# One over the softmax sum moves from each query tile into its head pair's gate, and GpSimd's work is pinned to written order

## The chip, the cores and the metric

One core of one Trainium2 chip. The metric is device time in microseconds (us). Before: median 1193.33 us of 3 runs (1192.71 to 1193.87). Below, a tile is 128 queries of one head.

## What is computed

A two-layer trunk on x (1024 x 1024) with 256 memory tokens; each layer ends in x <- LayerNorm(alpha * x + W_out [main * silu(gate); mem * silu(gate)]). The change lies in layer 1, where main is forgetting attention (16 heads of width 64):

```
logits = einsum(q, k) * scale + (cum[t] - cum[s])      # cum: running sum of the log forget gates
p = softmax(where(s <= t, logits, -inf))               # per head, 8 blocks of 128 queries
main = p @ v                                           # per head, 1024 x 64
y = concat(main * silu(g_main), mem * silu(g_mem)) @ w_out
```

The factor 1/sum of the softmax belongs to a query of a head. It may be put on p before `p @ v`, or on the rows of main, or on the gate that multiplies main.

## The kernel before

Every f32 product on TensorE (PE) is made from 16-bit halves: a high half and a low half (the rest). The profile's name PE is TensorE, DVE is VectorE, ACT is ScalarE, POOL is GpSimd, SP issues most DMAs.

**The attention stage** (`fox`, about 636 to 1068 us of the span) walks 16 heads in pairs, and in each head 8 tiles, number 7 (1024 columns) down to number 0 (128 columns). Tiles 7 to 4 have two parts of at most 512 columns (a and b below), tiles 3 to 0 have one. One tile runs so:

- PE: two matmuls for each part (L321) write the logits into a bank of PSUM called L; there are three of these banks, taken in turn.
- DVE: one instruction for each part (L1007; the profile shows it as CUSTOM_DVE_ANT_0 and its reader, `order` lists print ISA) adds the forget rows R or a masked copy of them (raw), takes the row extremum, and frees the bank L.
- ACT: the exponential (L1015), with the row sum as a second output, into PSUM (tag T, two banks).
- DVE: `inverse_of`, 1/sum: L1025 or L1027 (a 128x1 tensor_scalar), then L1028 (a 128x1 reciprocal).
- ACT: the high half e/sum (L1043), which needs that 1/sum; DVE: the low half (L1044), which needs the high half.
- SP: DMA transposes of the halves (`turn`, L1060); six tiles later (LAG) PE multiplies them with the values (L1069), after every fourth tile (52 matmuls at i = 1 of the next head, 20 at i = 5), and ACT (L1086) and DVE (L1087) put the result into the pair's output tile G.

The instructions of one engine start in its order, so an instruction that waits holds all that stand behind it. DVE's order: the inverse of a tile is written behind the next tile's first part, its low halves behind the next tile's last part; a scheduler moves them from there.

**Fill.** Between logits and values PE gets matmuls of projections (L353, "slabs" of 48 matmuls of 512 columns: the next pair's keys, queries, values, and gates), spread evenly over the tiles of a pair by `Fill.pump`: PE should always have something to do. A slab's weights come by a 512 KB DMA into a tile B; GpSimd scales them (L174) and makes the halves (L191 high, L176 low), 512 columns at a time, two times a slab. The first step of a unit (its DMA) is asked when the unit before it begins.

**GpSimd** also makes the masked copies of the forget rows (L981, three tiles ahead), and multiplies a pair's output with its gate (`pair_out`, L1096, four of 128x256; `late_gate`, L1109, for pairs 3, 5, 6, whose gates are made late). Its order is the scheduler's.

**The last pair** (heads 14 and 15) has pieces of the output projection in its fill, whose halves are split by ACT (L196) and DVE (L197).

Of the kernel before, what the change touches and what calls it, by code (L numbers as in the profile page):

```python
# [9 lines left out]
F32 = mybir.dt.float32  # L10
# [32 lines left out]
class Fill:  # L43


    def __init__(self):
        self.units, self.left, self.due, self.early = [], 0, 0, []

    def add(self, units, cols, early=False):
        self.units.append(units)  # L50
        self.left += cols
        if early:
            self.early.append(units)

    def pump(self, cols):

        self.due += cols
        while self.due > 0 and self.units:
            if len(self.units) > 1 and self.units[1] in self.early:
                self.early.remove(self.units[1])  # L60
                next(self.units[1])
            n = next(self.units[0], None)
            if n is None:
                self.units.pop(0)
            else:
                self.due -= n
                self.left -= n
        if not self.units:
            self.due = self.left = 0
# [8 lines left out]
def trunk_kernel(ctx, tc, x, xT, memT, win, wk, wv0, wv, wmk, wmv, wout, poolw, pscale, lng, lnb, bforget, out):  # L78
# [94 lines left out]
    def gp_scaled_hi_lo(to, src, sc):  # L173
        nc.gpsimd.tensor_scalar(src, src, sc, 1.0, ALU.mult, ALU.mult)  # L174
        gp_copy(to.hi, src)
        nc.gpsimd.tensor_tensor(to.lo, src, to.hi, ALU.subtract)  # L176
# [146 lines left out]
    def slab(pieces_dram, X, evac, banks=("pj", 2), g=0):  # L323
# [9 lines left out]
        ws = list(pieces_dram) if arrived else [split_w(pieces_dram[0], [P, 4, P], sc, both[0])]  # L333
        accs = {}
# [455 lines left out]
    with tc.tile_pool(name="in1", bufs=1) as in1:  # L790
# [165 lines left out]
        def start_units(own, following):  # L956
# [11 lines left out]
            yield from islice(following, 48)  # L968
# [8 lines left out]
        def mask(hd, i, R):  # L977
# [3 lines left out]
            nc.gpsimd.affine_select(  # L981
                C[:, :w], R[:, lo:up], [[-1, w]], ALU.is_ge, -NEG, base=w - P, channel_multiplier=1,
            )
# [8 lines left out]

# [38 lines left out]
        joined = []  # L1031

        def halves(hd, i, es, r):

            L = (i + 1) * P
            if i in (2, 0):
                pair = joined.pop()[:, 2 * L + 2 * P :]
            else:
                pair = sb([P, 2 * S], "P", 4, F16)
                if i in (3, 1):  # L1040
                    joined.append(pair)
            for lo, up, e in es:
                nc.scalar.activation(pair[:, lo:up], e, AF.Copy, scale=r)  # L1043
                nc.vector.scalar_tensor_tensor(pair[:, L + lo : L + up], e, r, pair[:, lo:up], ALU.mult, ALU.subtract)  # L1044
            return hd, i, pair
# [46 lines left out]
        def pair_out(pr, c, o, g):  # L1092

            for k in (2 * c + 1, 2 * c) if g is not None else ():
                cols = slice(k * 2 * P, (k + 1) * 2 * P)
                nc.gpsimd.tensor_tensor(o[:, cols], o[:, cols], g[:, cols], ALU.mult)  # L1096
# [3 lines left out]
        def late_gate(pr):  # L1100
# [6 lines left out]
            for c in range(4):  # L1107
                cols = slice(c * 2 * P, (c + 1) * 2 * P)
                nc.gpsimd.tensor_tensor(o[:, cols], o[:, cols], g[:, cols], ALU.mult)  # L1109
            nc.sync.dma_start(y1d[pr // 4, :, pr % 4, :], o)  # L1110

        def fox(following, out_proj):
            fill, past, fresh = Fill(), [None] * LAG, [None]
            gs = {}
# [3 lines left out]

            def gate_ahead(pr):
                gs[pr] = G()  # L1120
                fill.add(gate_units(win[1, 12 + pr], gs[pr], X, 2), SLAB, True)
# [4 lines left out]
            for hd in range(HEADS + 1):  # L1126
# [3 lines left out]
                if hd < HEADS:  # L1130
                    if b == 0:
                        o, sums = G(), sb([P, 4 * ST], "sums", 2, F32, small).rearrange("p (n b i) -> p n b i", n=2, b=2)
                        if 0 < pr < 7:
                            for units in (k_units, q_units, v_units):
                                fill.add(units(pr + 1), SLAB, True)
                        for ahead in {0: (0, 1), 2: (2,), 4: (4,), 7: (7,)}.get(pr, ()):
                            gate_ahead(ahead)
                            if ahead == 0:
                                fill.add(following, SLAB)
                        for late in (3, 5, 6) if pr == 7 else ():  # L1140
                            fill.add(late_gate(late), SLAB, True)
                    R, ahead_R = ahead_R, None
                for i in range(ST if hd < HEADS else LAG):
# [7 lines left out]
                    def inverse():  # L1151
                        if fresh[0]:
# [3 lines left out]
                    def behind():  # L1156
                        if fresh[0]:
                            split.append(halves(*fresh[0]))
# [18 lines left out]
                    if hd < HEADS:  # L1177
                        new = (hd, tile_of, o)
                        fresh[0] = probs(hd, tile_of, R, sums, inverse, behind)
                    else:  # L1180
# [95 lines left out]
```

## Time and profile before

| | |
|---|---|
| runs | 1192.71, 1193.33, 1193.87 us |
| profiled execution, its own time | 1197.14 us |
| its span | 1195.3 us |
| PE busy | 1169.2 us, 98% of the span |
| DVE busy | 788.1 us, 66% |
| ACT busy | 685.2 us, 57% |
| GpSimd busy | 286.4 us, 24% |
| mean granted PE clock | 0.993 |

The profiled execution is 3.8 us above the median of the runs, and 1.8 us longer than its span. A busy engine is shown by the time of its instructions; matmuls overlap in the pipe, so the mean duration of one is longer than the distance between two. "Waited for" is idle time of an engine put down to the instruction that ended it.

### The profile page before, as it was taken

Reading aid. Unit: us, or ns where it says so; the run is one execution under the profiler, and the core shown is the slowest. Engines: PE = TensorE matmul, PEld = TensorE weight load, DVE = VectorE, ACT = ScalarE, POOL = GpSimd, SP = SyncE. Lnnn points to the kernel's source line nnn. Section 1 sums busy time; section 2 is a strip of 40 time slices with the busy share of each in tenths; the row PEclk is TensorE's granted clock in tenths of the full one; section 3 lists DMA queues with packets and bytes.
Section 4 is the critical chain, followed back from the end, with each engine's and each line's share of the span. In section 5 each row is a group of like instructions: output and inputs, shape, how many; then the busy total and the mean of one; then the engine's idle time right before and its main releaser. Section 6 shows DMA issues by size and latency. Waiting matters only on the chain. (4 is left out here: it accounts for less than half of the span.)

```text
span 1195.3 us, 19795 instructions
## 1 busy us (share of the span) xinstructions
PE 1169.2 (98%) x6941; PEld 673.1 (56%) x6941; DVE 788.1 (66%) x1840; ACT 685.2 (57%) x1512; POOL 286.4 (24%) x437
## 2 busy tenths in 40 slices
PE   8999999999999999999999999999999999999996
PEld 5556776555555557556674555555555545455553
DVE  6744675556765566447755888778877788874654
ACT  6468875966563234557431776666766667674210
POOL 3321001220000000010224454545434331750000
PEclk8999999999999999999999999999999999999999
DMA  7566557655286544446734889989996999785430
GB/s 259 167 228 210 152 115 214 222 190 159 88 281 169 146 134 121 136 130 125 179 146 121 185 181 210 206 173 189 209 185 139 168 193 206 201 195 174 173 109 36
DMA packets 286195, 203.88 MB, mean 171 GB/s; under 512 B 224912, under 2 KB 238352, under 8 KB 286096
## 3 DMA queue, kind: packets, MB, share of 16 engines
q1 hardware_dynamic: 279696, 181.59, 61.0%
q0 software_dynamic: 6400, 21.04, 5.4%
q8 instruction: 54, 0.88, 0.3%
q14 instruction: 45, 0.37, 0.1%
HBM read 116.01 MB, written 22.61 MB: 116 GB/s over the span
## 5 line engine op out<-in xcount | busy, mean ns | idle before, releaser
L353 PE MATMUL pj<-A,w 128*128 128x512 f16 (+2 forms) x2896 | 665.1, 383 | 2.8 <-DMA A<-A 1.1
L353 PEld LDWEIGHTS <-w 128*128 128x128 f16 (+1 forms) x2560 | 246.2, 98 | 280.3 <-issue 12.8
L1015 ACT ACTIVATE T<-MK,s 128x512 f32<-128x512 f32 x192 | 111.2, 579 | 66.5 <-DVE s L1007 50.0
L1044 DVE SCALAR_TENSOR_TENSOR P<-T,s,P 128x512 f16<-128x512 f32 x192 | 112.0, 613 | 39.4 <-ACT P L1043 38.2
L1043 ACT ACTIVATE P<-T,s 128x512 f16<-128x512 f32 x192 | 103.0, 576 | 53.5 <-issue 28.9
L174 POOL TENSOR_SCALAR B<-B,scales 128x512 f32<-128x512 f32 x54 | 39.5, 742 | 376.1 <-PE pj L353 262.5
L593 PEld LDWEIGHTS <-T 128*128 128x128 bf16 x736 | 70.8, 98 | 87.4 <-issue 4.4
L981 POOL TENSOR_SCALAR_AFFINE_SELECT raw<-R 128x256 f32<-128x256 f32 (+3 forms) x128 | 59.8, 469 | 132.8 <-DVE s L1007 70.8
L321 PE MATMUL L<-A 128*128 128x512 f16 (+3 forms) x384 | 84.8, 326 | 6.1 <-DVE s L1007 6.1
L197 DVE TENSOR_TENSOR w<-raw,w 128x512 bf16<-128x512 f32 x74 | 52.4, 709 | 56.3 <-ACT w L196 39.3
L353 PEld LDWEIGHTS pj<-A,w 128*128 128x128 f32 x352 | 65.2, 188 | 17.8 <-ACT w L196 2.3
L197 DVE TENSOR_TENSOR T<-T,T 128x1024 bf16<-128x1024 f32 x23 | 28.0, 1220 | 68.0 <-PE pj L593 38.3
L321 PEld LDWEIGHTS <-A 128*128 128x128 f16 x384 | 37.4, 98 | 49.4 <-issue 8.0
L176 POOL TENSOR_TENSOR w<-B,w 128x512 f16<-128x512 f32 x54 | 63.3, 1173 | 2.7
L196 ACT CAST w<-raw 128x512 fp32r<-128x512 f32 x76 | 46.7, 615 | 24.8 <-DMA raw<-in_win_dram 11.7
L196 ACT CAST T<-T 128x1024 fp32r<-128x1024 f32 x23 | 24.1, 1047 | 62.5 <-DMA T<-y1d 34.3
L1069 PEld LDWEIGHTS <-V 128*64 128x64 f16 (+1 forms) x1152 | 50.6, 104 | 12.9 <-issue 6.0
L1069 PE MATMUL O<-T,V 128*64 128x128 f16 (+1 forms) x1152 | 57.5, 220 | 0.0
L593 PE MATMUL pj<-B,T 128*128 128x512 bf16 (+1 forms) x192 | 53.0, 384 | 0.0
L1007 DVE CUSTOM_DVE_ANT_0 MK<-L,R,scales 128x512 f32<-128x512 f32 x64 | 45.3, 708 | 9.6 <-PE L L321 9.3
L198 ACT CAST w<-raw 128x512 bf16<-128x512 f32 x78 | 48.2, 618 | 5.7 <-PE pj L353 4.3
L593 PE MATMUL L<-B,T 128*128 128x512 bf16 (+1 forms) x168 | 47.3, 394 | 0.2 <-ACT T L198 0.2
(286 smaller groups left out, 1815.2 us busy)
## 6 DMA issues: line engine op xcount, KB each, us to landing
raw<-in_win_dram SPq DMA_DIRECT2D x66, 256.0 KB, 3.6
W<-in_win_dram POOLq DMA_DIRECT2D x48, 256.0 KB, 3.9
R<-cumd SPq DMA_DIRECT2D x16, 512.0 KB, 4.6
B<-in_win_dram SPq DMA_DIRECT2D x15, 512.0 KB, 4.5
y0d<-Y SPq DMA_DIRECT2D x12, 512.0 KB, 3.8
raw<-in_wout_dram SPq DMA_DIRECT2D x24, 256.0 KB, 2.7
T<-y0d SPq DMA_DIRECT2D x12, 512.0 KB, 4.5
A<-A SPq DMA_DIRECT2D x24, 256.0 KB, 4.5
```

The costliest lines, as they stand in the source:

```text
L176: nc.gpsimd.tensor_tensor(to.lo, src, to.hi, ALU.subtract)
L196: pin(nc.scalar.copy(to.hi, src))
L197: pin(nc.vector.tensor_tensor(to.lo, src, to.hi.bitcast(F32), ALU.subtract))
L198: pin((top or nc.scalar.copy)(to.top, src))
L321: nc.tensor.matmul(acc, a, b, start=i == 0, stop=i == len(terms) - 1)
L353: nc.tensor.matmul(accs[n], a[:, k, :], b[:, pc * 4 + k, n * NH : (n + 1) * NH], start=seen[n] == 1, stop=seen[n] == 3 * KT,)
L593: nc.tensor.matmul(accs[a][nh], y, w, start=kt == 8 and i == 0, stop=kt == 7 and i == 2,)
L981: nc.gpsimd.affine_select(C[:, :w], R[:, lo:up], [[-1, w]], ALU.is_ge, -NEG, base=w - P, channel_multiplier=1,)
L1015: nc.scalar.activation(e, p[:, lo:up], AF.Exp, bias=top, scale=-1.0, accum_out=sums[:, n, hd % 2, i : i + 1],)
L1043: nc.scalar.activation(pair[:, lo:up], e, AF.Copy, scale=r)
L1044: nc.vector.scalar_tensor_tensor(pair[:, L + lo : L + up], e, r, pair[:, lo:up], ALU.mult, ALU.subtract)
L1069: nc.tensor.matmul(acc[rows, (i % 4) * P : (i % 4) * P + P], v[:, b, 2 * j : 2 * j + (1 if e else 2), :].rearrange("p e d -> p (e d)"), pt ...
```

## The change

- **1/sum.** Heads 0 to 13 (pairs 0 to 6) no longer call `inverse_of`. The high half is e times a constant (PSCALE, 2^15), made by ACT at once behind the exponentials; the low half uses the same constant. So the pair's output is not yet divided by its sums. In the next pair's even head the sums of the pair (16 columns of 128) are added (L1072) and inverted (L1073) on DVE, transposed by PE into a bank of L (L1077), copied (L1079) and written to DRAM (8 KB, L1080); two reads (L1083) spread them over 64 partitions each, into a B tile I of 128 x 1024. GpSimd multiplies gate and I (L1236, four of 128x256) for pairs 0, 1, 2, 4; for pairs 3, 5, 6 I takes the place of the gate in `pair_out`, which had no product there before.
- **`pair_out`** and its write to DRAM move from the odd head's values to tile i = 7 of the next pair's even head. The last pair keeps its 1/sum in the tiles and its `pair_out` at the values.
- **GpSimd** keeps written order for masks, weight halves and products.
- **Weights** are asked in three stages (DMA; halves of the first 512 KB half; of the second), when the unit in front has 48 matmuls left, 30, and 16. The keys of the pair after the next (or gate 7) are asked in the odd head at i = 2, 5 and 6; gate 0 ahead of the stage.

GpSimd has 382 rows instead of 355 in its order, DVE 1550 instead of 1753, SP 480 instead of 469, and PE 7 matmuls (with their weight loads counted apart) more; the order of PE is otherwise the same.

```diff
     def pump(self, cols):
...
-            if len(self.units) > 1 and self.units[1] in self.early:
-                self.early.remove(self.units[1])
-                next(self.units[1])
-            n = next(self.units[0], None)
+            if len(self.units) > 1 and self.units[1][2]:
+                behind, ahead = self.units[0][1], self.units[1]
+                while ahead[2] > (2 if behind > 30 * NH else 1 if behind > 16 * NH else 0):
+                    next(ahead[0])
+                    ahead[2] -= 1
...
     def gp_scaled_hi_lo(to, src, sc):
-        nc.gpsimd.tensor_scalar(src, src, sc, 1.0, ALU.mult, ALU.mult)
-        gp_copy(to.hi, src)
-        nc.gpsimd.tensor_tensor(to.lo, src, to.hi, ALU.subtract)
+        pin = tc.keep_in_program_order
+        pin(nc.gpsimd.tensor_scalar(src, src, sc, 1.0, ALU.mult, ALU.mult))
+        pin(gp_copy(to.hi, src))
+        pin(nc.gpsimd.tensor_tensor(to.lo, src, to.hi, ALU.subtract))
...
+        def inverse_columns(sums):
+            nc.vector.tensor_tensor(sums[:, 0, :, 4:], sums[:, 0, :, 4:], sums[:, 1, :, 4:], ALU.add)
+            nc.vector.reciprocal(sums[:, 0], sums[:, 0])
+
+        def inverse_rows(pr, sums):
+            t = ps([P, NH], "L", 3)[: 2 * ST, :P]
+            nc.tensor.transpose(t, sums[:, 0].rearrange("p b i -> p (b i)"), ident)
+            rows = land([P, P])[: 2 * ST]
+            nc.vector.tensor_copy(rows, t)
+            nc.sync.dma_start(invd[2 * pr : 2 * pr + 2].rearrange("h (s q) -> (h s) q", s=ST), rows)
+            I = land([P, S])
+            for b in range(2):
+                nc.sync.dma_start(I[64 * b : 64 * b + 64], invd[2 * pr + b].partition_broadcast(64))
+            return I
...
                     def inverse():
-                        if fresh[0]:
+                        if fresh[0] and fresh[0][0] >= HEADS - 2:
...
+                    if b and pr < 7 and i in (2, 5, 6):
+                        if i == 2:
+                            head = k_units(pr + 2) if pr < 6 else gate_of(7)
+                        next(head)
...
                         fresh[0] = probs(hd, tile_of, R, sums, inverse, behind)
+                        if pr < 7:
+                            es = fresh[0][2]
+                            fresh[0] = hd, tile_of, es, PSCALE, high_halves(tile_of, es, PSCALE)
+                        if b == 0 and pr:
+                            if i == 0:
+                                inverse_columns(whole)
+                            if i == 1:
+                                I = inverse_rows(pr - 1, whole)
+                            if i == 6:
+                                g = gs.get(pr - 1)
+                                for k in range(4) if g is not None else ():
+                                    cols = slice(k * 2 * P, (k + 1) * 2 * P)
+                                    tc.keep_in_program_order(
+                                        nc.gpsimd.tensor_tensor(g[:, cols], g[:, cols], I[:, cols], ALU.mult))
+                                gs[pr - 1] = I if g is None else g
...
                         values(older[0], older[1] // 4, older[2])
-                        if older[0] % 2:
-                            pair_out(older[0] // 2, older[1] // 4, older[2], gs.get(older[0] // 2))
+                        if older[0] == HEADS - 1:
+                            pair_out(7, older[1] // 4, older[2], gs[7])
+                        elif older[0] % 2 and older[1] == 0:
+                            done = older[2]
+                    if b == 0 and i == 7:
+                        for c in (1, 0) if pr else ():
+                            pair_out(pr - 1, c, done, gs[pr - 1])
```

Two places of the order. First, DVE in head 2 (the even head of pair 1), from tile 6's second part to tile 5's second part; MK is the tile's logits, P holds the halves of tile 7, G the output of the pair before. Before:

```order
L1007 ISA MK_7056,s_7057<-L_7065,raw_6945,s_7057,scales 128x384
L1007 ISA s_7057 128x1
L1025 TENSOR_SCALAR s_7062<-sums_7004 128x1
L1028 RECIPROCAL s_7062<-s_7062 128x1
L1044 SCALAR_TENSOR_TENSOR P_7069<-T_7024,s_7062,P_7069 128x512
L1044 SCALAR_TENSOR_TENSOR P_7069<-T_7026,s_7062,P_7069 128x512
L1087 SCALAR_TENSOR_TENSOR G_6357<-O_7081,scales,G_6357 64x512
L1007 ISA MK_7142,s_7143<-L_7144,R_6688,scales 128x512
L1007 ISA s_7143 128x1
L1025 TENSOR_SCALAR s_7148<-sums_7004 128x1
L1007 ISA MK_7142,s_7143<-L_7151,raw_6973,s_7143,scales 128x256
```

The same piece in the changed kernel (L1024 is L1007's line there, L1067 is L1044's, L1128 is L1087's); P_6991 is tile 7, P_7034 tile 6:

```order
L1079 COPY B_7039<-L_7037 16x128
L1024 ISA MK_7018,s_7019<-L_7024,raw_6918,s_7019,scales 128x384
L1024 ISA s_7019 128x1
L1067 SCALAR_TENSOR_TENSOR P_6991<-T_6987,P_6991 128x512
L1067 SCALAR_TENSOR_TENSOR P_6991<-T_6989,P_6991 128x512
L1024 ISA MK_7107,s_7108<-L_7109,R_6676,scales 128x512
L1024 ISA s_7108 128x1
L1067 SCALAR_TENSOR_TENSOR P_7034<-T_7030,P_7034 128x512
L1128 SCALAR_TENSOR_TENSOR G_6369<-O_7048,scales,G_6369 64x512
L1024 ISA MK_7107,s_7108<-L_7113,raw_6944,s_7108,scales 128x256
```

The two inverses are gone; the values' L1128 now stands behind tile 5's first part, and tile 6's first low half (P_7034) stands between tile 5's two parts.

Second, GpSimd in pair 2, in the last three tiles of head 4, changed kernel. The raw rows are masks of head 5's tiles 7, 6 and 5; B_7930 is the values' weights of pair 3, w_7990 and w_8032 their halves; G_6371 is pair 1's gate, B_7753 its I, G_6970 its output:

```order
L1002 AFFINE_SELECT raw_7946<-R_7723 128x512
L1002 AFFINE_SELECT raw_7997<-R_7723 128x384
L176 TENSOR_SCALAR B_7930<-B_7930,scales 128x512
L1236 TENSOR_TENSOR G_6371<-G_6371,B_7753 128x256
L193 TENSOR_SCALAR w_7990<-B_7930 128x512
L1236 TENSOR_TENSOR G_6371<-G_6371,B_7753 128x256
L178 TENSOR_TENSOR w_7990<-B_7930,w_7990 128x512
L1236 TENSOR_TENSOR G_6371<-G_6371,B_7753 128x256 x2
L176 TENSOR_SCALAR B_7930<-B_7930,scales 128x512
L193 TENSOR_SCALAR w_8032<-B_7930 128x512
L1002 AFFINE_SELECT raw_8039<-R_7723 128x256
L178 TENSOR_TENSOR w_8032<-B_7930,w_8032 128x512
```

Before, in the same three tiles of head 4 (raw_8025, raw_8083 and raw_8119 are the masks of head 5's tiles 7, 6, 5). B_8178 is the weights of gate 2, which head 5's last tiles use; B_8577 those of pair 4's keys, used from head 6 on; B_10399 the values' weights of a later pair; G_7003 is pair 1's output, G_6360 its gate:

```order
L981 AFFINE_SELECT raw_8025<-R_7799 128x512
L176 TENSOR_TENSOR w_8445<-B_8178,w_8445 128x512
L981 AFFINE_SELECT raw_8083<-R_7799 128x384
L174 TENSOR_SCALAR B_10399<-B_10399,scales 128x512 x2
L1096 TENSOR_TENSOR G_7003<-G_7003,G_6360 128x256 x2
L981 AFFINE_SELECT raw_8119<-R_7799 128x256
L191 TENSOR_SCALAR w_8579<-B_8577 128x512
L981 AFFINE_SELECT raw_8155<-R_7799 128x256
L176 TENSOR_TENSOR w_8579<-B_8577,w_8579 128x512
```

Before, the halves in the queue at these tiles are those of the next slab but one and later ones; now they are those of the next slab (the values of pair 3, whose first matmuls stand in head 5's first tile), with the four new products of a gate between them.

More of the change, by code (lines that the diff above doesn't have):

```diff
@@ L954, in pair_units, with gate_of, ask, start_units @@
                 yield from v_units(p)
-        def start_units(own, following):
+        gs = {}
+        def gate_of(pr):
+            gs[pr] = G()
+            return gate_units(win[1, 12 + pr], gs[pr], X, 2)
+        def ask(units):
+            low[0] = True
+            next(units)
+            low[0] = False
+        def start_units(own, following, gate):
             yield from v_first()
```

77 lines of the change are left out of this document (46 added, 31 removed).

## The prediction, made blind

> **What bounds the kernel now.** I read the page's busy shares first, then the table of PE's waits for the whole run, then the same table for the attention stage alone (640 to 1030 us), and at last the timelines of the engines around two of the waits. The page's row of busy times, and the first row of PE's waits (total us, times, longest):
>
> ```profile
> PE 1169.2 (98%) x6941; PEld 673.1 (56%) x6941; DVE 788.1 (66%) x1840; ACT 685.2 (57%) x1512; POOL 286.4 (24%) x437
> PE L L321 <- DVE s L1007: 6.1, 7, 2.5
> ```
>
> PE is busy for 98% of the span (1195.3 us); no other engine passes 66%. So time on DVE, ACT or GpSimd counts only where PE waits for it. The largest such sum is that of the logits for a free bank L: 6.1 us in 7 waits, the longest 2.5. Nothing else that the change touches is among PE's waits of any size. The same table for the stage up to head 14:
>
> ```profile
> PE L L321 <- DVE s L1007: 3.5, 6, 1.1
> POOL raw L981 <- DVE s L1028: 47.8, 28, 4.3
> ```
>
> Six waits, 3.5 us, lie there; the seventh, 2.5, lies in the last pair. Now one of the six, in head 2 at 704 us: DVE, then ACT, then PE (start and duration in us; in brackets the idle time before and what ended it).
>
> ```profile
> 699.44 0.67 DVE L1007 CUSTOM_DVE_ANT_0 MK<-L,raw,s 128x384 f32<-128x384 f32 x1
> ...
> 700.40 0.21 DVE L1025 TENSOR_SCALAR s<-sums 128x1 f32<-128x1 f32 x1 [0.29 <-ACT T L1015]
> 700.65 0.16 DVE L1028 RECIPROCAL s<-s 128x1 f32<-128x1 f32 x1
> 701.90 1.41 DVE L1044 SCALAR_TENSOR_TENSOR P<-T,s,P 128x512 f16<-128x512 f32 x2 [1.08 <-ACT P L1043]
> 703.34 0.76 DVE L1087 SCALAR_TENSOR_TENSOR G<-O,scales,G 64x512 f32<-64x512 f32 x1
> 704.13 0.75 DVE L1007 CUSTOM_DVE_ANT_0 MK<-L,R,scales 128x512 f32<-128x512 f32 x1
> ...
> 699.55 0.69 ACT L1015 ACTIVATE T<-MK,s 128x512 f32<-128x512 f32 x1 [0.42 <-DVE P L1044]
> 700.18 0.19 ACT L1015 ACTIVATION_READ_ACCUMULATOR T<-MK,s 128x1 f32 x1
> 701.18 1.27 ACT L1043 ACTIVATE P<-T,s 128x512 f16<-128x512 f32 x2 [0.81 <-ACT T L1015]
> 702.47 0.68 ACT L1086 ACTIVATE G<-O,scales 64x512 f32<-64x512 f32 x1
> ...
> 701.41 2.54 PE L353 MATMUL pj<-A,w 128*128 128x512 f16 x11
> 703.78 0.49 PE L321 MATMUL L<-A 128*128 128x384 f16 x2
> 704.94 0.38 PE L321 MATMUL L<-A 128*128 128x256 f16 x2 [0.67 <-DVE s L1007]
> ...
> 707.32 0.59 PE L321 MATMUL L<-A 128*128 128x512 f16 x2
> ```
>
> Tile 4's second part (704.94, 256 columns) needs the bank that tile 5's first part gives back at 704.81 (DVE's row at 704.13 with its reader). That row stands on DVE behind tile 7's low halves (701.90), they behind the high halves on ACT (701.18), and these behind 1/sum (700.40 and 700.65). ACT was done with the exponentials at 700.37 and stood 0.81 us for 1/sum; DVE stood 1.08 for ACT. So 1/sum is in the chain that PE waits for.
>
> What a wait costs: 11 fill matmuls take 2.54 us, and one lasts about 0.38, so they follow each other at (2.54-0.38)/10 = 0.216. Two of 384 columns need 2 x 0.162 us; PE could have gone on at 703.78+0.32 = 704.10 and did at 704.94. That is 0.84, 0.17 more than the row's 0.67. The six waits cost **3.5 + 6 x 0.17 = 4.5 us**.
>
> **What goes.** 112 tiles lose a reciprocal, 56 of them an L1025 and 56 an L1027:
>
> ```profile
> L1028 DVE RECIPROCAL s<-s 128x1 f32<-128x1 f32 x121 | 19.6, 162 | 2.6
> L1025 DVE TENSOR_SCALAR s<-sums 128x1 f32<-128x1 f32 x61 | 12.9, 211 | 17.2 <-ACT T L1015 16.8
> L1027 DVE TENSOR_SCALAR s<-sums 128x1 f32<-128x1 f32 x60 | 9.1, 151 | 10.9 <-ACT T L1015 10.4
> ```
>
> That is 112 x 0.162 + 56 x 0.211 + 56 x 0.151 = 38.4 us of DVE, and the idle time behind it. Beside PE's 98% it counts nothing by itself; it counts through the six waits. In head 2: ACT's high halves can start at 700.37 in place of 701.18; with one of 0.63 the first low half starts at 701.0, and the two end at 702.4. L1087 stands behind tile 5's first part now, so that part runs from 702.4 to 703.2. PE wants the bank at 704.10: 0.9 us to spare, and the wait is gone. The other five have the same form. In the odd heads of pairs with four slabs, tile 6's first low half stands ahead of tile 5's first part as well, so I take five sixths: **-3.7 us** (ends 0 and -4.5).
>
> **What is late next.** Behind tile 5's first part now come the first low half of tile 6, L1087, and tile 5's second part, whose bank tile 3 wants (PE at 707.32, without the 0.84 at 706.5). The low half needs tile 6's exponentials and high half, L1087 needs ACT's L1086, which ACT has behind tile 6's high halves. Walked with these rows: ACT's exponentials of tile 6 from 701.7 (tile 7's first low half ends) to 703.2, high halves to 704.5, L1086 to 705.2, L1087 to 705.9, the second part (0.55) to 706.5. Tile 7's second exponential itself waited 0.42 (699.55) for a low half of the head before, which comes earlier now. So the bank comes 0 to 0.5 us before PE wants it. I take that as no wait, but it is the forecast's weakest point.
>
> **What PE gets.** Seven transposes of 128 columns (L1077). Before has one of that kind, and the same two DMAs as the new ones, for the running sums:
>
> ```profile
> L891 PE MATMUL T<-ident,G x1: 272/272/272, 640.0 to 640.0; 128*128 128x128 f32 x1
> L891 PEld LDWEIGHTS T<-ident,G x1: 140/140/140, 639.8 to 639.8; 128*128 128x128 f32 x1
> cumd<-G SPq DMA_DIRECT2D x1, 64.0 KB, 1.5
> R<-cumd SPq DMA_DIRECT2D x16, 512.0 KB, 4.6
> ```
>
> One costs PE at most 0.272+0.140 = 0.41 us; at least, if it flows like fill, a quarter of 0.216, 0.05. I take the weight load's 0.14, since the load is not hidden by a matmul of its length: 7 x 0.14 = **+1.0** (ends 0.4 and 2.9). It stands behind tile 6's logits and takes the bank of tile 7's second part, which DVE has read by then. The new add, reciprocal and copy are 21 DVE instructions where 224 go: nothing, while DVE is not the bound. Write and reads take 1.5 + 4.6 us; five tiles of about 3 us lie between them and the products on GpSimd. SP's 11 further issues stand between loads that are asked a slab ahead.
>
> **GpSimd.** The written order puts a slab's scaling, halves and the gate products of a pair together. The rows of before for each:
>
> ```profile
> L176 POOL TENSOR_TENSOR w<-B,w 128x512 f16<-128x512 f32 x51 | 59.9, 1174 | 2.5
> L191 POOL TENSOR_SCALAR w<-B 128x512 f16<-128x512 f32 x50 | 30.8, 617 | 23.1 <-PE pj L353 22.9
> L174 POOL TENSOR_SCALAR B<-B,scales 128x512 f32<-128x512 f32 x32 | 22.2, 702 | 45.4 <-DMA B<-in_win_dram 19.8 <-DMA B<-in_wv_dram 14.1 <-DMA B<-in_wk_dram 11.5
> L981 POOL TENSOR_SCALAR_AFFINE_SELECT raw<-R 128x256 f32<-128x256 f32 x46 | 18.3, 399 | 47.5 <-DVE s L1007 21.1 <-DVE s L1028 17.0 <-DVE s L1027 9.4
> L1096 POOL TENSOR_TENSOR G<-G,G 128x256 f32<-128x256 f32 x16 | 11.3, 726 | 6.6 <-DVE G L1087 6.6
> ```
>
> The tightest place that I found is the one quoted with the change, in pair 2: for both halves of the values' weights two scalings, two high and two low halves, four products and a mask of 256, 2 x (0.70+0.62+1.17) + 4 x 0.73 + 0.40 = 8.3 us. By PE's order, from head 4's tile 1 to the second half's first use stand 14, 13 and 12 fill matmuls and logits worth about 1.2 us: 39 x 0.216 + 1.2 = 9.6 us. So 1.3 to spare; the first half has more. I cost the pinning at **0** (cover: those 1.3 us; without it, see the second rival). No gain: weights are no wait of PE's in this stage now. 28 more products x 0.73 = 20 us for GpSimd, which had the room.
>
> **The last pair** keeps 1/sum in its tiles, and in head 15 DVE's order is the old one. Its wait and what follows (the last row is a window of 4 us, with the busy time of PE, weight loads, DVE, ACT and GpSimd, then the granted clock, 0.57):
>
> ```profile
> 1033.48 1.88 DVE L197 TENSOR_TENSOR MK<-A,MK 128x512 bf16<-128x512 f32 x1
> ...
> 1036.73 0.59 PE L321 MATMUL L<-A 128*128 128x256 f16 x2 [2.52 <-DVE s L1007]
> 1037.11 4.51 PE L353 MATMUL pj<-A,w 128*128 128x512 f16 x14
> ...
> 1036.00:1040.00 4.00, 3.27 (x10) 1.37 (x10) 3.95 (x12) 1.31 (x4) 0.69 (x2) 0.57 0.59 202
> ```
>
> After 2.52 us of idleness the granted clock was 0.57 from 1036 to 1040, which costs another 4.0 x 0.43 = 1.7 us; I leave all of it in: **0**. [...]
>
> **The sum**, on the profiled execution: 1197.14 - 3.7 + 1.0 = 1194.4. It is 3.8 us above the runs' median, and I take the difference to hold; so 1193.33 - 2.7 = **1190.6**.
>
> **Rivals.**
> - *The wait moves* (same). Tile 3 waits for tile 5's second part, now that a low half and L1087, which waits for ACT's L1086, stand ahead of it. For: the half microsecond above. Against: DVE has 38 us less to do. If it takes back 2 to 3.7 of the gain, 1192.6 to 1194.3. From 0.5 us of lateness in a head on it decides.
> - *GpSimd's queue holds the weights back* (slower). A mask waits for DVE up to 4.3 us (the row of L981's waits above), and now no half can pass it. If that falls on a place with 1.3 to spare, PE waits 3.0 and loses the clock as at 1036, 1.7: 4.7 a place. One place gives 1190.6 + 4.7 = 1195.3, two 1200.0. It decides from 1.3 us of delay on. For: halves stood a slab and more ahead, now just ahead. Against: GpSimd is busy for 24% of the span, and what a mask waits for, DVE's reading, comes earlier now.
> - *The last pair's wait goes too* (faster yet): DVE's queue enters pair 7 with less behind it, or L197 is not held: -2.5 -1.7, 1186.4.
> - That the change doesn't do what it says is not a case here: the order shows the inverses gone.
>
> **How the numbers follow.** Forecast 0.42, the wait moves 0.26, GpSimd 0.22, the last pair too 0.10. The forecast's own range is 1189.8 (-3.5) to 1192.5: by more than 0.2% (2.4 us, about what a measurement of this kernel can tell from no change) faster in two thirds of it. Faster: 0.42 x 2/3 + 0.10 = 0.38. Same: 0.14 + 0.19 = 0.33. Slower: 0.22 + 0.07 = 0.29. The range reaches from the third rival's 1186 to one and a half places on GpSimd, 1190.6 + 7.0 = 1197.6.
>
> **What would show it.** Right: PE's waits for L at DVE's row shrink to one or two before head 14, none in head 2; no wait of ACT's high halves for DVE; seven transposes under 0.3 us each of PE. Wrong: a wait of PE's fill for a half made by GpSimd, with clock below 1.00 behind it (second rival); a wait of single-part tiles (128x512) for a bank (first); the span of 1036 to 1068 shorter (third).

## The result, and the profile after

The changed kernel takes 1206.71 us (median of 5 runs, 1206.21 to 1214.35); before 1193.51 (5 runs). The ratio is 1.0125, 95% interval 1.0106 to 1.0143: **13.2 us slower**, where 2.7 faster was forecast and 1197.6 was the end of the range. The profiled execution has 1206.21 us, a span of 1204.4.

Before's profiled execution reached the attention stage 6.4 us later than after's; over all kernels of this study the stage begins between 644 and 652 us, whatever they change. So the stage is compared by itself, from PE's first logits matmul to the last tile's. Four rows of PE's timeline, two of before and two of after:

```profile
651.56 1.03 PE L321 MATMUL L<-A 128*128 128x512 f16 x4
...
1051.48 0.28 PE L321 MATMUL L<-A 128*128 128x128 f16 x2
```

```profile
645.11 1.03 PE L323 MATMUL L<-A 128*128 128x512 f16 x4
...
1060.45 0.28 PE L323 MATMUL L<-A 128*128 128x128 f16 x2
```

399.9 us before, 415.3 after: **+15.4 us**; the loss lies in this stage (what follows it takes 143.8 us before and 144.0 after). Below, "stage" is this length in a run's profile.

The page's busy times and the table of PE's waits after (whole run; us, times, longest):

```profile
PE 1168.1 (97%) x6900; PEld 673.5 (56%) x6948; DVE 753.1 (63%) x1637; ACT 669.8 (56%) x1512; POOL 304.7 (25%) x465
```

```profile
PE L L323 <- issue: 6.6, 2, 4.9
PE L L323 <- DVE P L1067: 3.0, 1, 3.0
PE L L323 <- DVE s L1024: 2.7, 1, 2.7
PE pj L359 <- POOL w L193: 1.8, 1, 1.8
...
PE L L323 <- ACT MK L816: 1.2, 1, 1.2
PE L L1077 <- DVE s L1024: 1.0, 2, 0.6
```

DVE has 35 us less to do, as the change meant. The six waits for a bank L before head 14 are gone: the row of DVE's s holds one wait, 2.7, the last pair's. But the logits wait four times for something else, under three names. The place quoted from before, head 2 from tile 6's second part on, runs now like this (DVE, then ACT, then PE):

```profile
692.24 0.68 DVE L1024 CUSTOM_DVE_ANT_0 MK<-L,raw,s 128x384 f32<-128x384 f32 x1
...
692.84 1.28 DVE L1067 SCALAR_TENSOR_TENSOR P<-T,P 128x512 f16<-128x512 f32 x2
694.82 0.75 DVE L1024 CUSTOM_DVE_ANT_0 MK<-L,R,scales 128x512 f32<-128x512 f32 x1 [0.69 <-PE L L323]
...
691.05 0.67 ACT L1032 ACTIVATE T<-MK,s 128x512 f32<-128x512 f32 x1
...
691.76 1.06 ACT L1060 ACTIVATE P<-T 128x512 f16<-128x512 f32 x2
...
691.46 0.27 PE L1077 MATMUL L<-ident,sums 128*16 128x128 f32 x1
...
699.91 0.59 PE L323 MATMUL L<-A 128*128 128x512 f16 x2
```

ACT goes from the exponentials to the high halves with no gap, DVE waits for PE instead of PE for DVE. That part of the plan works. The four waits (start of the first logits of heads 4, 8, 12 and 14), and the windows behind two of them (the third number from the end is the granted clock):

```profile
735.27 1.02 PE L323 MATMUL L<-A 128*128 128x512 f16 x4 [1.72 <-issue]
...
842.42 1.86 PE L323 MATMUL L<-A 128*128 128x512 f16 x4 [2.96 <-DVE P L1067]
...
948.08 1.02 PE L323 MATMUL L<-A 128*128 128x512 f16 x4 [1.24 <-ACT MK L816]
...
999.08 1.86 PE L323 MATMUL L<-A 128*128 128x512 f16 x4 [4.91 <-issue]
```

```profile
841.00:846.00 5.00, 3.58 (x11) 1.33 (x12) 3.01 (x8) 1.81 (x6) 0.40 (x2) 0.66 1.07 201
998.00:1003.00 5.00, 3.92 (x11) 1.46 (x12) 2.09 (x5) 0.74 (x3) 0.61 (x1) 0.66 1.01 223
```

Each is the first tile of a pair. The names "issue", DVE and ACT mislead: all three had long been done. The tile reads the pair's queries, and in each of the four cases the last of the three copies that put them in place (`move`, L909; L903 before) landed 0.1 us before PE went on. From start to start of the matmuls, as the prediction counted it, the four cost 1.9 + 3.1 + 1.4 + 5.1 = 11.5 us. In the two windows the clock is 0.66 (0.50 from 842 to 845 and from 999 to 1002), which is 3.4 us at half speed or 1.7 us each: 3.4. Together 14.9, against the 15.4 of the stage. The smaller terms nearly cancel: the six waits that are gone (-4.5) against PE's wait for a weight half (L193, 1.8), the seven transposes and their waits (0.8 + 1.0) and a wait of the fill (0.9).

Why the copy is late shows on SP. Its queue before and after, ahead of head 4 (SP's DMAs as issued: start, time that the issue took):

```profile
709.72 0.82 SPq L988 DMA_DIRECT2D R<-cumd  x1
711.73 1.28 SPq L1060 DMA_TRANSPOSE T<-P  x1
714.62 0.37 SPq L330 DMA_DIRECT2D B<-in_win_dram  x1
...
717.44 1.42 SPq L903 DMA_DIRECT2D A<-A  x2
718.96 5.62 SPq L1060 DMA_TRANSPOSE T<-P  x2
724.69 0.53 SPq L903 DMA_DIRECT2D A<-A  x1
```

```profile
707.04 0.58 SPq L1009 DMA_DIRECT2D R<-cumd  x1
707.67 0.42 SPq L332 DMA_DIRECT2D B<-in_wk_dram  x1
708.19 1.13 SPq L909 DMA_DIRECT2D A<-A  x2
709.42 6.09 SPq L1101 DMA_TRANSPOSE T<-P  x1
...
717.13 0.47 SPq L909 DMA_DIRECT2D A<-A  x1
...
719.22 1.39 SPq L332 DMA_DIRECT2D B<-in_win_dram  x1
720.71 5.57 SPq L1101 DMA_TRANSPOSE T<-P  x2
...
727.50 1.11 SPq L909 DMA_DIRECT2D A<-A  x2
728.70 2.13 SPq L1101 DMA_TRANSPOSE T<-P  x1
732.23 0.46 SPq L909 DMA_DIRECT2D A<-A  x1
```

Four things are to be seen. The forget rows R (512 KB), a load of weights (512 KB) and the moves of the keys are issued within 2.3 us now (707.04 to 709.32), where it was 9.1. A transpose behind them takes 6.09 us to issue, and holds the queue; the same transpose (tiles 3 and 2 of head 2) is the first of the two at 718.96 before, which took 5.62 together. The queries' last half was made by DVE at 724.5 (L913), but the queries' moves start at 727.50, 3.0 us later, since transposes and forget rows stand ahead of them; before, it was made at 732.3 (L907), and the move that reads it started at 732.91. And the third move, which overwrites what the first reads, waits for the first to land: the first, issued at 727.50, took 4.7 us to land, the third, issued at 732.23, another 3.0, one after the other. The three 256 KB moves of the keys took this long from issue to landing, before (window 706 to 727) and after (700 to 720):

```profile
A<-A SPq DMA_DIRECT2D x3, 256.0 KB, 5.0
```

```profile
A<-A SPq DMA_DIRECT2D x3, 256.0 KB, 8.0
```

### The profile page after: what moved, and what is told of

The parts are those of the page before. It is cut to its first block, busy times and chain, and to the rows that moved or that the text cites. A ratio compares the mean times of both kernels' runs of the same rounds, so it can differ in the third digit from the quotient of the medians.

```text
span 1204.4 us, 19629 instructions
## 1 busy us (share of the span) xinstructions
PE 1168.1 (97%) x6900; PEld 673.5 (56%) x6948; DVE 753.1 (63%) x1637; ACT 669.8 (56%) x1512; POOL 304.7 (25%) x465
## 5 line engine op out<-in xcount | busy, mean ns | idle before, releaser
L1067 DVE SCALAR_TENSOR_TENSOR P<-T,P 128x384 f16<-128x384 f32 (+1 forms) x168 | 90.6, 554 | 59.0 <-ACT P L1060 57.9
L323 PE MATMUL L<-A 128*128 128x512 f16 (+3 forms) x384 | 85.1, 331 | 13.6 <-issue 6.6
L199 DVE TENSOR_TENSOR w<-raw,w 128x512 bf16<-128x512 f32 x74 | 51.8, 701 | 52.9 <-ACT w L198 37.8
L1060 ACT ACTIVATE P<-T 128x384 f16<-128x384 f32 (+1 forms) x168 | 74.8, 478 | 17.8 <-DMA T<-P 16.3
L1024 DVE CUSTOM_DVE_ANT_0 MK<-L,R,scales 128x512 f32<-128x512 f32 x64 | 45.6, 713 | 40.2 <-PE L L323 38.3
L199 DVE TENSOR_TENSOR T<-T,T 128x1024 bf16<-128x1024 f32 x23 | 28.2, 1226 | 67.7 <-PE pj L599 39.2
L323 PEld LDWEIGHTS <-A 128*128 128x128 f16 x384 | 37.3, 98 | 57.3 <-issue 11.8
```

Of the source, the lines that this page charges most:

```text
L199: pin(nc.vector.tensor_tensor(to.lo, src, to.hi.bitcast(F32), ALU.subtract))
L323: nc.tensor.matmul(acc, a, b, start=i == 0, stop=i == len(terms) - 1)
```

## Experiments

The question after this: the change brings five things to SP's queue or moves them there (the asks for weights, the write of 1/sum, its two reads, the wait between them, `y1d`'s write), and the transposes start earlier. Which of them makes the moves late? In the diffs a minus is the changed kernel's line (of before's in `x3_before_sp_written`). Ratios are to runs of before on the same chip.

### One part alone, one part taken away

`e1_order_only` keeps GpSimd's written order and the staged asks and leaves 1/sum in every tile:

```diff
-                        if fresh[0] and fresh[0][0] >= HEADS - 2:
+                        if fresh[0]:
```

> GpSimd's written order and the weights asked in three stages, without the move of 1/sum (1/sum in every tile, pair_out at the values, as before). Theory A (loads asked in a bunch just ahead of use back up the DMA queues, and the moves of the next pair's queries land late): 1200 us or more, with PE waiting at the first tile of heads 4, 8, 12, 14. Theory B (the reads of 1/sum and the later write of the output are the traffic that is too much) and theory C (high halves made a tile earlier put transposes ahead of the moves in SP's order): within 2 us of before, 1193.5.

1193.45 us, ratio 0.999 [0.9977, 1.0003], stage 400.2. No change is seen: pinning and asks cost nothing by themselves.

`e2_sums_only` keeps the move of 1/sum, and takes GpSimd's order and the asks back to before's:

```diff
-        pin(gp_copy(to.hi, src))
-        pin(nc.gpsimd.tensor_tensor(to.lo, src, to.hi, ALU.subtract))
+        gp_copy(to.hi, src)
+        nc.gpsimd.tensor_tensor(to.lo, src, to.hi, ALU.subtract)
```

> The move of 1/sum alone: GpSimd's order left to the scheduler, weights asked as before. Theory A: 1190 to 1194, no wait of PE at the first tile of an even head. B and C: 1200 or more, with those waits.

1224.82 us, ratio 1.0248 [1.0218, 1.0277], stage 430.7, with waits of up to 7.8 us for the logits at the start of heads. So the move of 1/sum makes the loss, and GpSimd's new order and asks, far from being at fault, save 15 us of it (430.7 against 415.3).

`e3_no_spread` keeps all but the way through DRAM; the products take the pair's output in place of I, so 1/sum is missing from the result of heads 0 to 13:

```diff
-            nc.sync.dma_start(invd[2 * pr : 2 * pr + 2].rearrange("h (s q) -> (h s) q", s=ST), rows)
-            I = land([P, S])
-            for b in range(2):
-                nc.sync.dma_start(I[64 * b : 64 * b + 64], invd[2 * pr + b].partition_broadcast(64))
```

> The changed kernel without the write of 1/sum to DRAM and its two reads; GpSimd's products take the pair's output in place of the spread 1/sum, so their number and place stay (1/sum is left out of heads 0 to 13). Theory B: 1197 or less, the moves land in 5 us again. A and C: 1203 or more, moves still 8 us.

**1189.08 us, ratio 0.9955 [0.9939, 0.997], stage 397.0.** All that PE waits for in the stage, first at head 14, then in the last pair (640 to 1070 us):

```profile
PE L L323 <- issue: 2.4, 1, 2.4
PE L L323 <- DVE s L1024: 0.8, 1, 0.8
```

So the rest of the change makes the stage 2.9 us shorter (the whole run 5.4 by the medians on this chip). That this is near the forecast's -2.7 is luck, for it is made of other terms: the six waits are gone (-4.5), the last pair's wait is shorter and loses no clock (-3.5, which the forecast had left in), the transposes take 0.8, and the wait at head 14 with 3.4 us at half clock behind it (11 fill matmuls in 4.22 us, 2.54 ahead of the wait) gives 4.3 back. The write and the two reads, with the order of SP's queue that comes with them, cost 415.3 - 397.0 = 18.3 us (17.6 by the medians).

`e4_high_late` puts the high halves back to where they were:

```diff
-                            fresh[0] = hd, tile_of, es, PSCALE, high_halves(tile_of, es, PSCALE)
+                            fresh[0] = hd, tile_of, es, PSCALE
```

> The changed kernel with the high halves made at their old place, behind the next tile's logits, still with the constant. Theory C: 1197 or less, transposes and moves in the old order. A and B: 1203 or more.

1203.53 us, ratio 1.009 [1.0065, 1.0115], stage 410.2: 5 of the 15 us (3 by the medians). Transposes that come earlier are a third of the loss at most.

### What of the spread: bytes, wait, place

`e5_reads_free` takes the write away and reads the running sums, which need no wait; `e6_quarter_reads` reads 256 of 1024 columns; `e7_reads_late` asks the reads three tiles later; `e8_reads_gp` does so on GpSimd's DMA queue. The gates of e5 and e6, and of e9 and e11 below, lack the right 1/sum.

```diff
 e5
-                nc.sync.dma_start(I[64 * b : 64 * b + 64], invd[2 * pr + b].partition_broadcast(64))
+                nc.sync.dma_start(I[64 * b : 64 * b + 64], cumd[2 * pr + b].partition_broadcast(64))
 e6
+                nc.sync.dma_start(I[64 * b : 64 * b + 64, : 2 * P], invd[2 * pr + b, : 2 * P].partition_broadcast(64))
 e7 (e8 with nc.gpsimd in spread)
-                                I = inverse_rows(pr - 1, whole)
+                                inverse_rows(pr - 1, whole)
+                            if i == 4:
+                                I = spread(pr - 1)
```

> The changed kernel without the write of 1/sum, and with its two reads taken from the running sums' rows of the pair (same shape and bytes, landed long ago), so that no read waits; gates are multiplied by wrong rows. Theory D (the reads' bytes and packets on the DMA engines, 512 KB a pair, in tiles where these are full, make the moves late): 1203 or more. Theory E (SP stands for the write to land ahead of the reads, and transposes and moves behind it start late): 1192 or less.

> The changed kernel with write, wait and place as they are, but only the first 256 of 1024 columns read (128 KB a pair in place of 512); all four products use these columns, so the gates are wrong. D: a quarter of the traffic's 17.6 us, 1191 to 1196. E: 1203 or more.

> The changed kernel with the two reads asked at tile i = 4 in place of 1 (the write stays at 1), so that the write has landed. E: 1195 or less. D: 1203 or more, since the same bytes now fall nearer the moves of the keys.

> As the run with late reads, but the two reads are issued by GpSimd on its own DMA queue, so SP neither issues nor waits for them. D: 1200 or more (same bytes on the same engines). E: 1195 or less. If GpSimd's issue holds its weight halves back, PE waits for w and the run is slower by that.

Measured: e5 1194.11 (0.9994 [0.9979, 1.0009], stage 400.0), e6 1192.97 (0.9986 [0.9973, 0.9999], 400.5), e7 1209.38 (1.0129 [1.0108, 1.015], 413.5), e8 1202.78 (1.0071 [1.0049, 1.0094], 406.9). So the full bytes without a wait cost 3.0 us against e3, and a wait with a quarter of the bytes 3.5, where both together cost 18.3. Two reads fewer on SP's queue (e8) leave 9.9. What e5 and e6 still lose lies at head 14 (waits of 4.6 and 5.1 us, e3's was 2.4); at heads 4, 8 and 12 PE no longer waits. e5 met neither of its two expectations. e7 turned out to be no test: a scheduler sets SP's order, and it put the reads back to where they were.

Two more of this kind, `e11_wait_only` (reads of 16 columns) and `e9_write_no_wait` (write, and full reads of the running sums):

> The changed kernel with write, wait and two reads of 16 columns each (8 KB a pair in place of 512); products with the pair's output and one small product with what was read, so the gates are wrong. SP's order is that of the runs with quarter reads and with free reads but for a few rows. If the wait for the write costs: 1193, as with quarter reads. If the bytes do: 1189 to 1190.5.

> The changed kernel with the write, but its two full reads taken from the running sums, so that they wait for nothing; the gates are wrong. If the wait together with the bytes makes the loss: 1195 or less. If bytes and write do, or the place in SP's queue that they bring: 1203 or more.

1192.93 (0.9986 [0.9974, 0.9998], stage 400.8) and 1193.45 (0.9995 [0.9985, 1.0004], 402.3). Neither the wait by itself nor the bytes by themselves make the loss, and the pieces don't add up to it; as far as these runs go, it takes both together. That the wait is small shows in the changed kernel too, in what the reads stood for the write (us, times, longest, 640 to 1050 us):

```profile
SPq L1083 <- DMA invd<-B: 3.4, 3, 1.5
```

The programs show what else differs: the scheduler moved other DMAs of SP's in these kernels. Of the 245 DMAs from the first forget rows to the last transpose, e4 and e7 have 243 and 238 in the changed kernel's order, e3, e5, e6, e8 and e9 only 177 to 207. So these runs compare orders as much as pieces.

### SP's order by hand

To hold the order fixed, SP's DMAs of the stage were pinned as written: the changed kernel (`x1_sp_written`), the same without the spread (`x2_sp_written_no_spread`), and before (`x3_before_sp_written`).

```diff
-            nc.sync.dma_start_transpose(to[:, :n, :], two[:, : n * P])
+            tc.keep_in_program_order(nc.sync.dma_start_transpose(to[:, :n, :], two[:, : n * P]))
```

> The changed kernel, all of its work, bytes and waits as they are, but SP's loads, moves, transposes, spread and writes of the attention stage pinned to written order: a pair's keys are then moved ahead of the next load of weights, and the load of the next keys stands behind tile 7's transpose, no longer just ahead of the moves. Theory G (the place of the loads in SP's queue, which the write and the two reads push against the moves, decides): 1196 or less, moves of the queries 3 us and more ahead of PE. If the bytes themselves decide: 1203 or more.

> The same without the write and the two reads (1/sum left out of heads 0 to 13, products with the pair's output). By G the difference to the run with them is small, 5 us or less, the price of the bytes in a good order; if the bytes decide, 1189 and 14 us or more below it.

> The kernel before with SP's loads, moves, transposes and writes of the attention stage pinned to written order. A control: within 2 us of before by every theory; if it is faster by 3 us or more, the written order of SP is a gain of its own and not the cure of the change's loss.

1237.98 (1.0391 [1.0349, 1.0433]), 1218.88 (1.0211 [1.0187, 1.0235]) and 1304.58 (1.0924 [1.0894, 1.0954]). If the place of the loads were all, x1 would be at 1196 or less and x2 within 5 us of it; neither held, and before did not stay within 2 us. In a fixed order the spread costs 19.1 us too, which speaks for its bytes, but among other waits (weights, 18.9 us in x1, 6.5 in x2). The third number tells most: with no work added or taken away, the order of SP's queue alone is worth 111 us in before, 90.9 of them waits for weights.

### Which pairs can bear it

Next the room that the moves have, in each pair: the time from the landing of the queries' third move to the first logits that read them (from the trace, us; 0.1 is a wait of PE's):

| head | 2 | 4 | 6 | 8 | 10 | 12 | 14 |
|---|---|---|---|---|---|---|---|
| before | 2.7 | 4.7 | 16.5 | 3.8 | 16.7 | 4.6 | 4.2 |
| after | 5.0 | 0.1 | 9.8 | 0.1 | 12.6 | 0.1 | 0.1 |
| e3_no_spread | 5.0 | 2.2 | 16.9 | 1.6 | 17.4 | 1.3 | 0.1 |

Heads 6 and 10 have 10 us and more, since their pair's fill has a fourth slab (a gate) behind the queries. A spread is read in the even head of the pair after its own, and then the moves for the next pair follow. So the spreads of pairs 1 and 3 meet the moves for heads 6 and 10, which have room, and those of pairs 0, 2, 4 and 5 the moves that have not; behind that of pair 6 no moves follow. `m13_two_pairs` moves 1/sum for pairs 1 and 3 only, `m02456_five_pairs` for the five others:

```diff
-                        if pr < 7:
+                        if pr in SPREAD:
...
-                        if b == 0 and pr:
+                        if b == 0 and pr - 1 in SPREAD:
```

> The changed kernel with the move of 1/sum for pairs 1 and 3 alone (the others keep 1/sum in the tiles and pair_out at the values). Their spread is read in heads 4 and 8, in pairs with four slabs, where the moves of the queries are 10 us and more ahead of PE; heads 2, 3, 6, 7 lose their waits for 1/sum (2.2 us in before). If the price of the spread is what it makes of the moves' slack: 1190.5 to 1193, no wait at the first tile of an even head. If each spread costs its share wherever it stands (17.6/7 = 2.5 us): 1196 or more.

> The other five pairs alone: their spreads are read in heads 2, 6, 10, 12 and 14, four of them ahead of the even heads where PE waited. By the slack: 1203 or more. By shares: 5 x 2.5 above 1190, about 1202, so the run before this one decides between the two and this one shows where the waits stand.

m13: **1192.35 (0.9983 [0.9972, 0.9995]), stage 397.3**, near e3's 397.0 with no spread at all (one execution each, and m13's is the fastest of its twelve; by the ratios it lies 3.3 us above e3); room of 2.1, 14.2, 1.7, 14.9, 4.7 and 4.7 us ahead of heads 4 to 14. m02456: 1199.61 (1.0037 [1.0024, 1.005]), stage 404.7, room of 0.1 ahead of heads 12 and 14, where PE waits up to 5.4 us; 1203 or more was expected. Where the moves have room, the spread takes some 2.5 us of it (14.2 and 14.9 in m13, 16.9 and 17.4 in e3) and makes PE wait for no move. That it costs a wait wherever there is little room isn't shown: heads 4 and 8 of m02456 kept 1.9 and 0.4 us, and PE didn't wait there.

### The place of the loads

Last, the loads. In the changed kernel one load of weights stands just ahead of the moves of the keys (707.67 above) and one between them and those of the queries (719.22). `x5_loads_ahead` is the full change with the same bytes and a like wait for the write (4.4 us in all, 3.4 in the changed kernel); the loads of a pair's slabs are asked at its start, and they, the write and the reads keep their written order:

```diff
                         for units in (q_units, v_units) if 0 < pr < 7 else ():
-                            fill.add(units(pr + 1), SLAB, 3)
+                            units = units(pr + 1)
+                            next(units)
+                            fill.add(units, SLAB, 2)
```

> The changed kernel with its full write, wait and reads, but the loads of a pair's queries', values' and gate's weights asked at the pair's start, and kept in written order with the write and the reads on SP: these loads then stand ahead of the spread and none of them just ahead of the moves of the keys or the queries; transposes and moves are left to the scheduler. If the place of the loads in SP's queue makes the loss: 1189 to 1196. If wait and bytes together make it in any order: 1202 or more.

**1198.0 us (1.0033 [1.0021, 1.0045]), stage 405.7: 8.7 us of the median and 9.6 of the stage's 18.3 are gone.** That lies between the two expectations: the place of the loads is a part of it, not all, and the scheduler moved other DMAs here as well (some 195 of the 245 are in the changed kernel's order). PE in head 8 and head 14 of x5:

```profile
840.59 1.02 PE L323 MATMUL L<-A 128*128 128x512 f16 x4
...
993.73 1.87 PE L323 MATMUL L<-A 128*128 128x512 f16 x4 [4.84 <-issue]
```

The waits at heads 4, 8 and 12 are gone or under 0.4 us, on 0.1, 0.1 and 1.1 us of room. That of head 14 stays, with 6.8 us at half clock behind it (0.53 from 992 to 999). SP's waits for a landing ahead of a move (L909, 640 to 1050 us) fall from 18.6 us, the longest 5.0, to 11.6, the longest 2.1. (That sum alone decides nothing: it is 19.3 in m13, where PE waits for no move.)

`m13_loads_ahead` and `m5_pairs0to4_loads_ahead` are x5 with the spread for pairs 1 and 3, and for pairs 0 to 4:

```diff
+SPREAD = (0, 1, 2, 3, 4)
```

> Both in one: loads ahead, and the move of 1/sum for pairs 1 and 3 alone. If the run before is fast, 1189 to 1192; if it is slow, as two pairs alone, 1192.3, or above by the loads' price.

> Loads asked at a pair's start as in x5_loads_ahead, the 1/sum spread through DRAM for pairs 0 to 4 only; pairs 5 and 6 keep 1/sum in their tiles as before. Theory (the slack of the queries' third move behind a pair of three slabs decides): in x5_loads_ahead heads 14 and the last pair still waited for that move (5.0 us and 3.7 us, each with some 3.4 us at half clock behind it); without the spreads that are read in those pairs the wait at head 14 goes, some 6 to 9 us come off x5's 1198.0, less the two waits for 1/sum that come back (under 1 us each): 1189 to 1193 us. Rival (the spread costs by its bytes and issues in every pair alike): five of seven spreads leave most of x5's loss against the kernel without a spread (1189): 1195 to 1197 us.

1193.4 (0.9993 [0.998, 1.0006], stage 400.1) and 1193.46 (0.9997 [0.9988, 1.0005], stage 400.7). The wait at head 14 is gone in m5. These are PE's longest wait up to 1010 us, and then the longest in the stage's whole window (us, times, longest):

```profile
PE L L324 <- DVE s L1025: 1.1, 2, 0.8
```

```profile
PE pj L360 <- POOL w L194: 4.9, 2, 3.7
```

1193.46 lies 0.5 us above the theory's range (1189 to 1193) and 1.5 below the rival's (1195 to 1197, the spread costs in every pair alike). The waits decide between them: up to head 14 PE waits for no move, so five spreads cost next to nothing there, and what m5 loses is a new wait in the last pair, 3.7 us for the weights of a late gate: their load was issued at 1014.08, landed at 1019.06, and GpSimd stood 6.61 us for it. That expectation also took the 3.7 us in x5's last pair for the queries' move; it is a wait of the projections, not of the logits, and no slow clock follows it. m13 stays the best that computes everything, 1.7 us below before.

## Why the prediction was wrong, step by step

- **"Write and reads take 1.5 + 4.6 us; five tiles of about 3 us lie between them and the products ... SP's 11 further issues stand between loads that are asked a slab ahead": this step failed.** It priced the spread by its own landing against its own reader, and it took 11 further rows of SP's order, in which equal neighbours are merged, for issues: they are 21 (7 writes and 14 reads). GpSimd indeed never waited for it (the products' group, with 0.0 us of idle time before it):

```profile
L1236 POOL TENSOR_TENSOR G<-G,B 128x256 f32<-128x256 f32 x16 | 11.2, 726 | 0.0
```

  Who else uses SP's queue was named and then set at nothing. The runs put 18.3 us there: with the spread the loads and moves fall together, transposes behind them hold the queue for up to 6.09 us (709.42), and the queries' third move, which had 3.8 to 4.7 us to spare ahead of heads 4, 8, 12 and 14, comes after PE wants it. e3 shows that it is the spread and the order that it brings, m13 that no move is late where there is room, x5 that half of it goes when the loads stand elsewhere in SP's queue.
- **The waits for 1/sum, -3.7: right.** All six are gone (-4.5, the end of its range); in head 2 ACT goes on without a gap, as walked, and DVE stands 0.69 us for PE.
- **Seven transposes, +1.0: 1.8 with their waits**, inside its ends of 0.4 and 2.9. Their row (ns, least, median, most):

```profile
L1077 PE MATMUL L<-ident,sums x7: 270/273/273, 691.5 to 1005.3; 128*16 128x128 f32 x7
```

  The next matmul starts 0.11 us behind (691.46 and 691.57 in head 2), so 0.8 us for seven; two of them waited 1.0 in all for a bank, which the term didn't have.
- **GpSimd's pinning, 0: right** by e1 (1193.45), and with the moved 1/sum it and the asks are needed (e2). The second rival, weights held back, did come true at one place, PE's 1.8 us for L193 (and in m5 3.7), through late loads and not through a mask: GpSimd had stood 5.98 us for that load.
- **The last pair, 0: right**: 2.7 us of waiting (the row of L323 for DVE's s above), before 2.5, each with slow clock behind it (0.66 from 1046 to 1051 us, 0.57 before). On DVE, L199 (L197 before) stood ahead of that bank's row for 4.67 us at 1039.46, where it was 1.88; no run shows by itself what made it long. The third rival (this wait goes) did not come here; it did in e3.
- **The first rival** (the wait moves to tile 3) was the weakest point of the forecast, and didn't happen: no single-part tile waits for a bank.
- **The slow clock behind a wait** was costed by the row of before (0.57 from 1036 to 1040, behind 2.52 us). The runs bear the row out: here 2.96 us of waiting had 0.66 behind them, from 841 to 846.

The sum without the failed step, -2.7, is close to e3's stage (-2.9) by luck, as shown there. What was missing was a rival on SP's queue; the room of each move could have been read from the trace of before (the first row of the table above) and set against the queue's new issues.

**Open.** Why wait or bytes alone cost 3 to 5 us and all together 18 isn't settled piece by piece: each kernel got another order of SP's queue, and pinning all of it cost far more than what was to be measured. How the scheduler comes to put the loads there was not tried. x5 shows that their place matters, not that it is all. 8.7 us are left in its stage against e3: 4.1 at head 14 (5.0 of waiting and 3.4 for 6.8 us at half clock, in e3 2.6 and 1.7), and 4.3 in the last pair, where x5 waits 3.5, 1.2 and 0.4 us and e3 0.8.

## What to carry to other kernels

Here a write of 8 KB and two reads of 256 KB a pair, which landed in 2.3 and 4.1 us (medians), cost 18.3 us with the order of SP's queue that came with them. So price a small transfer not by its own time alone: find the transfers in its queue with the least room (landing to first use, here 3.8 to 4.7 us), above all chains in which one copy waits for another to land (5.4 us of SP's waits before, 18.6 after), and ask whether the new issues go ahead of them. A scheduler may move other transfers when one is added (in e3, e5, e6, e8 and e9 177 to 207 of the 245 kept the changed kernel's order); compare the order of the DMA queue, not only of the engines. And where an edit is repeated over stages with different slack, apply it first where the room is, as `m13_two_pairs` did (1192.35 us).

## What the runs showed of the hardware

- The length of a wait doesn't by itself decide whether PE's clock drops. The wait ahead of the same matmuls in the last pair lasted 2.05 us in both e1 and m13_two_pairs; behind it the clock was 0.57 for 4 us in the one and 1.00 in the other (e1, then m13: the matmuls, and a window of 4 us):

```profile
1035.09 0.50 PE L323 MATMUL L<-A 128*128 128x256 f16 x2 [2.05 <-DVE s L1024]
1035.00:1039.00 4.00, 3.91 (x12) 1.60 (x12) 3.58 (x13) 1.96 (x6) 0.78 (x3) 0.57 1.28 232
```

```profile
1030.39 0.38 PE L324 MATMUL L<-A 128*128 128x256 f16 x2 [2.05 <-DVE s L1025]
1030.00:1034.00 4.00, 3.60 (x18) 1.76 (x18) 3.88 (x13) 1.97 (x6) 0.48 (x2) 1.00 1.04 243
```

  Waits of 2.4 us (e3) and 2.96 and 4.91 (after) were followed by 3.4 us at half clock, 4.84 us (x5) by 6.8, and 1.72 and 1.24 (after) by none (1.00 from 734 to 739 and from 947 to 952); but in x5's last pair 3.5 us of waiting were followed by none at all. That wait ends at 1045.2; the window behind it has a granted clock of 1.00:

```profile
1045.00:1050.00 5.00, 3.64 (x17) 1.59 (x18) 2.96 (x7) 3.27 (x8) 4.83 (x9) 1.00 1.09 208
```

- A DMA transpose of 384 KB occupied SP's queue for 1.28 us, 2 us behind one 512 KB copy (711.73 in before), one of 448 KB for 6.09 us right behind 1.5 MB of loads and copies (709.42 in after), and held all that stood behind it. The 6.09 hold no wait for its data: PE and the DMAs whose semaphores it waits for were done before it started (704.8).
